# Input projection of a two-layer hybrid block on one core: seven block products for eight on half of the contraction, convolved q and k through DRAM

## The chip, the cores and the metric

The kernel runs on one core of a Trainium2 chip. The metric is the device time of one execution in microseconds. Before the change three runs gave 1715.57, 1718.47 and 1721.88 us, median 1718.47 us.

## The reference, cut to what matters

Two layers are computed. In each, 1024 latent tokens and 256 context tokens (width 1024) are normalised and modulated, then multiplied by one input projection whose columns feed three groups: bidirectional gated DeltaNet heads (q, k, v, each through a 5-tap convolution over the tokens and a SiLU), latent attention heads, and a short convolution branch. Outputs are gated, concatenated and sent through one output projection.

```python
hx = modulate(x, norm_g, shift_x, scale_x)
hc = modulate(ctx, norm_g, shift_c, scale_c)
(xq, xk, xv, xz_a, xb, xa, xq_a, xkv_a, xz_b, xh, xbg, xcg, xz_c) = split_in(hx @ w_in)
(cq, ck, cv, cz_a, cb, ca, cq_a, ckv_a, cz_b, ch, cbg, ccg, cz_c) = split_in(hc @ w_in)
...
qkv = jax.nn.silu(dwconv_centred(jnp.concatenate([q, k, v], axis=-1), conv_w))
...
c_x = conv_branch(xh, xbg, xcg, xz_c, conv_w)
```

All of it is float32. The second layer computes context tokens only where keys, values and k are needed.

## The kernel before

**Operands.** A float32 product is made of three products of rounded parts (hi·hi, hi·lo, lo·hi). The tokens stand transposed in `hg` as hi and lo, in three groups (`GROUPS`: 512, 512 and 256 tokens), with the contraction of 1024 as 8 tiles of 128 (`KD`). The weights come in blocks of 128 output columns: `load_w` fetches one block (512 KB), `split_w` makes its hi on ScalarE (`split`, L75) and its lo on VectorE (L76).

**Blocks.** After 10 small tiles for the narrow columns (`mla_tile`) and two gate blocks (`z2`), `run_blocks` goes through a list `bl` of 24 blocks: k (4 heads), q (4), the convolution branch (2 x 4 parts: h, c gate, b gate, z), v (4), and four gate blocks. `Block.mm(g)` runs 24 matmuls into one PSUM bank for a token group; `post0` takes the banks (copy into a padded row `pad`, convolution `conv` as one ScalarE and four VectorE passes, SiLU), and `post1`, two blocks later, transposes the heads and stores them. Weight tiles `w` have two buffers (tag W8); the next but one block is split while the next is multiplied. Convolved q and k of all heads stay in SBUF (`KQ`).

**Background lanes.** Beside the blocks run generators on the kernel's own clock `Sched`: each 8 matmuls advance it by `tick(0.0034 * n)`, and a lane is resumed when its next due time has passed, so that a `yield` is rounded up to the next tick. `start_prep` (hook at block 4) makes the decay matrices and k·k per token tile, `start_base` (5) inverts small blocks in a long run of small VectorE operations (L680, L681), `start_prep_q` (9) makes q·k, `start_merge` (8) assembles inverses in ten `merge` generators on two workers, and `start_kv` (21) prepares the latent keys, `kv_lane`, once all ten are merged. The block phase ends at

```python
sch.until(lambda: len(kvf) == NT)
```

(L1037), after which the attention phase is written, with TensorE's order fixed by hand: the key rows are spread by DMA (`key_rope`, L1058), and attention (`a_max`, `a_scores`, `a_pv`) is interleaved with the two recurrences `recur`, whose inputs come through a DMA ring, while q and k are read from `KQ`. Outside that stretch the order on each engine comes from a planner that takes what is ready by its place in the program; every DMA is issued by SyncE (SP) in order.

**Buffers.** Tags share slots: B16 (7), B4 (2), W8 (2), T5 (5 rows of 1288), P4 (4), P2 (7); PSUM has 8 banks (`bank`). A tile whose tag has no free slot waits for one.

## Time and profile before

| | before |
|---|---|
| median of three runs | 1718.47 us |
| profiled execution | 1723.55 us, span 1721.8 us |
| mean granted TensorE clock | 0.978 of 2.4 GHz |
| busy share: TensorE, VectorE, ScalarE, GpSimd | 96%, 64%, 44%, 38% |
| block phase, first layer | 121 to 552 us of the span |
| block phase, second layer | 1000 to 1378 us |

The first stretch of the span loads and modulates the tokens, and after each block phase come attention with the recurrences (552 to about 815 us and 1378 to about 1622 us) and the output projection. A busy share is an average over these stretches. A matmul's listed duration overlaps its neighbours', so the pace of matmuls is read from chains of them and not from the mean duration.

### The profile page before, as it was taken

How to read it: one execution, taken by the hardware profiler on the slowest of the kernel's cores; microseconds unless marked ns; L12 is line 12 of the kernel's file. 1: busy time of each engine (PE TensorE's matmuls, PEld its weight loads, DVE VectorE, ACT ScalarE, POOL GpSimd, SP SyncE). 2: the span in 40 equal slices, each digit the busy share in tenths (PEclk: the TensorE clock that was granted, in tenths of full speed). 3: DMA queues.
4: the chain of work that ended last, by engine and by line, in shares of the span. 5: the costliest groups of instructions: out<-in, count | busy, mean ns of one | idle time of the engine just before them, and what ended most of it. 6: DMA issues, size and time to landing. Idle time of an engine off the chain costs nothing.

```text
span 1721.8 us, 29896 instructions
## 1 busy us (share of the span) xinstructions
PE 1650.5 (96%) x10964; PEld 1316.9 (76%) x10964; DVE 1101.9 (64%) x2041; ACT 758.8 (44%) x1909; POOL 646.3 (38%) x848
## 2 busy tenths in 40 slices
PE   7999999999999999998999999999999989999998
PEld 5887888787887877764888887787778778776586
DVE  2534668878643767765565346689797377776664
ACT  4644565223444534344354435652245444434432
POOL 0520345321320456557331212544232136556731
PEclk8999999999999899999999999999999989999999
DMA  9332464753254755544443314556524465454551
GB/s 360 124 126 79 155 196 150 242 178 123 78 160 125 257 157 177 186 144 159 132 141 111 104 56 134 161 179 224 166 70 128 151 211 164 160 188 156 172 159 49
DMA packets 195403, 266.54 MB, mean 155 GB/s; under 512 B 50529, under 2 KB 115249, under 8 KB 195257
## 3 DMA queue, kind: packets, MB, share of 16 engines
q1 hardware_dynamic: 195256, 264.64, 47.8%
q8 instruction: 87, 1.43, 0.3%
q14 instruction: 60, 0.48, 0.1%
HBM read 182.71 MB, written 79.17 MB: 152 GB/s over the span
## 4 chain that ended last, share of the span: by engine, by line
PE 68%; DVE 10%; DMA 9%; issue 5%; ACT 3%; POOL 3%; SPq 1%; POOLq 0%; DVEq 0%; ACTq 0%
PE bank L452 26%; PE bank L84 22%; PE bank L1159 3%; PE bank L1236 2%; PE bank L1255 2%; PE bank L1249 2%; DVE pr L680 2%; PE bank L1254 2%; PE bank L1102 2%; DMA gcb<-row_d 2%; DVE Mb L681 1%; DMA wa<-in_w_ada_dram 1%; PE bank L1226 1%; DVE acc L466 1%; PE bank L516 1%
## 5 line engine op out<-in xcount | busy, mean ns | idle before, releaser
L452 PE MATMUL bank<-h_hi,w 128*128 128x512 f32 x1664 | 432.5, 403 | 2.4 <-DVE h_hi L283 2.4
L452 PEld LDWEIGHTS bank<-h_hi,w 128*128 128x128 f32 x1664 | 305.4, 190 | 74.6 <-issue 4.5
L452 PE MATMUL bank<-h_lo,w 128*128 128x512 f32 x832 | 217.7, 402 | 0.0
L452 PEld LDWEIGHTS bank<-h_lo,w 128*128 128x128 f32 x832 | 154.3, 189 | 37.0 <-issue 1.6
L466 DVE SCALAR_TENSOR_TENSOR acc<-pad,col,acc 128x1284 f32<-128x1284 f32 (+1 forms) x104 | 160.1, 1540 | 11.1 <-ACT acc L463 9.5
L1129 POOL TENSOR_TENSOR vt<-vt,probT 128x512 f32<-128x512 f32 x110 | 144.7, 1335 | 20.2 <-ACT probT L1143 19.5
L84 PE MATMUL bank<-wo_hi,mix 128*128 128x512 f32 x576 | 145.0, 402 | 1.8 <-ACT wo_hi L75 1.1
L1143 ACT ACTIVATE probT<-bank 128x512 f32<-128x512 f32 (+1 forms) x168 | 96.5, 590 | 98.2 <-PE bank L84 92.2
L84 PEld LDWEIGHTS bank<-wo_hi,mix 128*128 128x128 f32 x576 | 108.2, 191 | 28.6 <-ACT wo_hi L75 2.6
L76 DVE TENSOR_TENSOR w<-wr,w 128x1024 fp32r<-128x1024 f32 x52 | 66.6, 1283 | 93.3 <-ACT w L75 93.3
L1104 DVE TENSOR_REDUCE mx<-bank 128x1 f32<-128x512 f32 (+1 forms) x200 | 108.5, 585 | 10.9 <-PE bank L1102 9.7
L452 PE MATMUL bank<-h_c,w 128*128 128x256 f32 x816 | 109.7, 287 | 0.0
L452 PEld LDWEIGHTS bank<-h_c,w 128*128 128x128 f32 x816 | 102.2, 190 | 5.8 <-issue 3.7
L75 ACT ACTIVATE w<-wr 128x1024 fp32r<-128x1024 f32 x52 | 54.9, 1060 | 75.3 <-PE bank L452 56.3
L84 PE MATMUL bank<-qt,kh 97*128 97x512 f32 (+1 forms) x256 | 84.4, 411 | 3.5 <-ACT probT L1143 2.8
L1159 PE MATMUL bank<-probT,vt 128*64 128x512 f32 (+1 forms) x336 | 79.4, 594 | 0.0
L1232 POOL TENSOR_TENSOR ring<-ring,qx 128x512 f32<-128x512 f32 x32 | 40.9, 1277 | 92.7 <-DMA ring<-row_d 76.8
L680 DVE TENSOR_TENSOR pr<-L,Mb 128x31 f32<-128x31 f32 (+15 forms) x186 | 70.7, 380 | 4.6
L84 PE MATMUL bank<-wo_lo,mix 128*128 128x512 f32 x288 | 73.5, 395 | 0.0
L681 DVE TENSOR_TENSOR Mb<-Mb,pr 128x31 f32<-128x31 f32 (+15 forms) x186 | 68.6, 369 | 5.0
L617 POOL TENSOR_TENSOR gcb<-gcb,gc 128x1024 f32<-128x1024 f32 x20 | 44.5, 2231 | 62.7 <-DMA gcb<-row_d 36.8
L79 ACT ACTIVATE pad<-bank 128x512 f32<-128x512 f32 (+1 forms) x78 | 41.0, 531 | 54.1 <-PE bank L452 39.1
(310 smaller groups left out, 3225.2 us busy)
## 6 DMA issues: line engine op xcount, KB each, us to landing
wr<-in_w_blk_dram SPq DMA_DIRECT2D x52, 512.0 KB
wa<-in_w_ada_dram SPq DMA_DIRECT2D x32, 512.0 KB
gcb<-row_d SPq DMA_DIRECT2D x20, 512.0 KB
nn_d<-N SPq DMA_DIRECT2D x20, 512.0 KB
ring<-vr_d SPq DMA_DIRECT2D x40, 256.0 KB
ring<-nn_d SPq DMA_DIRECT2D x40, 256.0 KB
qk_d<-gcb SPq DMA_DIRECT2D x18, 512.0 KB
ring<-kt_d SPq DMA_DIRECT2D x36, 256.0 KB
```

What stands on the lines that cost most here:

```text
L75: A.activation(out=hi, in_=raw, func=ACTF.Copy)
L76: eng.tensor_tensor(out=lo, in0=raw, in1=hi.bitcast(F32), op=ALU.subtract)
L84: T.matmul(outp, lhsT=lh, rhs=rh, start=q == 0, stop=q == n - 1)
L452: T.matmul(pb[:, 0:n], lhsT=self.w[:, wi, k, :], rhs=hg[g][hi][:, k, :], start=q + k == 0, stop=q == 2 and k == KD - 1)
L466: V.scalar_tensor_tensor(out=acc[:, 2:hi], in0=pad[:, 2 + t - r:hi + t - r], scalar=col[:, ci:ci + 1], in1=acc[:, 2:hi], op0=ALU.mult, op1 ...
L617: P.tensor_tensor(gcb, gcb, bc(gc[:, i, :], 128), ALU.subtract)
L680: V.tensor_tensor(out=pv, in0=bc(L[:, 0:k, k], w), in1=N[:, k:k + 1, k:32].to_broadcast([128, k, w]), op=ALU.mult)
L681: V.tensor_tensor(out=N[:, 0:k, k:32], in0=N[:, 0:k, k:32], in1=pv, op=ALU.subtract)
L1104: V.tensor_reduce(mx[:, gk:gk + 1], pb[:, 0:n], AX.X, ALU.max)
L1129: P.tensor_tensor(acc, a0, a1, ALU.add)
L1143: A.activation(out=pts[r][:, kk, 0:n], in_=pb, func=ACTF.Exp)
L1159: T.matmul(u["po"][64 * r:64 * r + 64, 0:n], lhsT=vx[:, kt, hh * 64:hh * 64 + 64], rhs=pts[r][:, kk, 0:n], start=kt == keys[0], stop=kt == ...
```

## The change

Blocks are taken in pairs (`run_pairs`). For token groups 0 and 1 and contraction tiles 0 to 3, the two blocks and two groups make a 2 by 2 by 2 block product, computed with seven products of 6 matmuls instead of eight. Sums of the tokens (`make_sums`, t1 to t4, in the slots of the narrow weights) are made once a layer, sums of the weights (`weight_sums`) once a pair; partial results go through PSUM banks and are added into SBUF rows (`add`, on VectorE, and two GpSimd adds). Tiles 4 to 7 and the context group stay as they were. A pair has three weight tiles (b0.w, ws, b1.w) in the two W8 slots; b0's lo is made on GpSimd, raw weights move to tag B4. The ticks are now `0.00255 * n` each 6 matmuls. Convolved q and k are stored to DRAM (`kx_d`, `qx_d`) and loaded again in `prep`, `prep_q`, before attention (`KQ`, two loads of eight tiles) and, for one step, in `recur`. The second merge worker starts only after all three base batches in both layers.

```diff
+        def weight_sums(a, b):
+            ws = st([128, 2, KD, 128], "W8", F32R, name="ws")
+            s1 = st([128, 2, 2, 128], "P2", name="sr")
+            s2 = st([128, 2, 2, 128], "P2", name="sr")
+            P.tensor_tensor(s1[:, 0], b[:, 0:2], b[:, 2:4], ALU.add)
+            P.tensor_tensor(s1[:, 1], s1[:, 0], a[:, 0:2], ALU.subtract)
+            P.tensor_tensor(s2[:, 0], a[:, 0:2], b[:, 0:2], ALU.subtract)
+            P.tensor_tensor(s2[:, 1], a[:, 2:4], s1[:, 1], ALU.subtract)
+            for q, s in enumerate((s1, s2)):
+                split(s.rearrange("p a b f -> p (a b) f"), ws[:, 0, 4 * q:4 * q + 4], ws[:, 1, 4 * q:4 * q + 4], P)
+            return ws
...
+        def run_pairs(blocks, hooks):
...
+                b0.open(b0.padded)
+                z = bank()
+                chain(z, prod(b0.w, 2, sm["b21"]) + b0.std(0))
+                copy_a(b0.dst(0), z)
+                ws = weight_sums(b0.raw, b1.wr)
+                b0.raw = None
+                if b0.n_tok == TOK:
+                    b0.mm(2)
+                x = bank()
+                chain(x, prod(b0.w, 0, sm["b11"]))
+                b0.add(0, x)
+                copy_a(b0.dst(1), x)
+                y = bank()
+                chain(y, b0.std(1), stop=False)
+                x = bank()
+                chain(x, prod(ws, 2, sm["t2"]))
+                b0.add(1, x)
+                with tc.high_priority(offset=300):
+                    b1.split()
...
+                chain(y, prod(ws, 6, sm["b22"]), False)
+                late(q - 1)
+                b1.open(b1.padded)
+                x = bank()
+                chain(x, prod(ws, 4, sm["t3"]))
+                b1.add(0, x, b0.dst(1))
+                b0.add(1, y)
+                x = bank()
+                chain(x, prod(ws, 0, sm["t1"]))
+                copy_a(b1.dst(1), x)
+                P.tensor_tensor(b0.dst(1), b0.dst(1), b1.dst(1), ALU.add)
+                P.tensor_tensor(b1.dst(1), b1.dst(1), b1.dst(0), ALU.add)
+                b0.post0(b0)
+                hook(q + 1)
+                if b1.n_tok == TOK:
+                    b1.mm(2)
+                y = bank()
+                chain(y, b1.std(0) + prod(b1.w, 2, sm["t4"]))
+                b1.add(0, y)
+                if nxt:
+                    with tc.high_priority(offset=300):
+                        nxt[0].raw = nxt[0].wr
+                        nxt[0].split(P)
+                else:
+                    load_qkv()
+                y = bank()
+                chain(y, b1.std(1))
+                b1.add(1, y)
+                late(q)
+                b1.post0(b1)
...
-                    if first or (len(based) >= (2 if last else 3) and free.ok("ada", "q")):
+                    if first or (len(based) == 3 and free.ok("ada", "q")):
...
+        for nm, src, n_kq in (("k", kx_d, 8), ("q", qx_d, 8)):
+            KQ[nm] = st([128, 8, 4, 128], "B16", name=nm + "x")
+            S.dma_start(out=KQ[nm], in_=src[0:8].rearrange("i p h t -> p i h t"))
         kh = st([128, 4, 1024], "B16", F32R, name="kh")
```

## Rows read from the trace of the kernel before

**Rows 1.** The page: busy time, share and instructions; then costliest groups.

```profile
PE 1650.5 (96%) x10964; PEld 1316.9 (76%) x10964; DVE 1101.9 (64%) x2041; ACT 758.8 (44%) x1909; POOL 646.3 (38%) x848
...
L452 PE MATMUL bank<-h_hi,w 128*128 128x512 f32 x1664 | 432.5, 403 | 2.4 <-DVE h_hi L283 2.4
...
L452 PE MATMUL bank<-h_lo,w 128*128 128x512 f32 x832 | 217.7, 402 | 0.0
...
L1129 POOL TENSOR_TENSOR vt<-vt,probT 128x512 f32<-128x512 f32 x110 | 144.7, 1335 | 20.2 <-ACT probT L1143 19.5
...
L76 DVE TENSOR_TENSOR w<-wr,w 128x1024 fp32r<-128x1024 f32 x52 | 66.6, 1283 | 93.3 <-ACT w L75 93.3
...
L75 ACT ACTIVATE w<-wr 128x1024 fp32r<-128x1024 f32 x52 | 54.9, 1060 | 75.3 <-PE bank L452 56.3
```

**Rows 2.** Both block phases: stretch, length, busy per engine, clock, DMA share, GB/s.

```profile
121.00:552.00 431.00, 424.46 (x3351) 344.89 (x3348) 279.33 (x481) 187.59 (x469) 119.49 (x187) 1.00 0.47 146
1000.00:1378.00 378.00, 367.30 (x2829) 294.90 (x2827) 266.52 (x458) 174.81 (x429) 118.14 (x189) 0.98 0.46 143
```

**Rows 3.** The chain that ended last: start, us, what.

```profile
555.04 5.30 DMA kc<-pes
...
957.41 9.33 PE bank L452 x40
...
1387.93 4.80 DMA ring<-nn_d
```

**Rows 4.** Second block phase in stretches of 10 us; columns as in rows 2.

```profile
1150.00:1160.00 10.00, 10.00 (x53) 8.42 (x52) 9.55 (x22) 3.90 (x17) 3.74 (x7) 1.00 0.64 194
...
1190.00:1200.00 10.00, 6.48 (x54) 5.30 (x53) 8.19 (x18) 3.53 (x8) 4.16 (x11) 0.71 0.56 172
...
1210.00:1220.00 10.00, 7.96 (x39) 6.67 (x39) 9.46 (x23) 1.53 (x3) 0.00 (x0) 0.66 0.39 116
```

**Rows 5.** VectorE in the first block phase (180 to 550 us), groups by shape.

```profile
L653 DVE TENSOR_TENSOR gcb<-bank,gcb 128x512 f32<-128x512 f32 x20 | 12.8, 681 | 0.1
```

**Rows 6.** VectorE in the second block phase, groups by shape.

```profile
L466 DVE SCALAR_TENSOR_TENSOR acc<-pad,col,acc 128x1284 f32<-128x1284 f32 x32 | 49.6, 1551 | 5.1 <-ACT acc L463 4.5
L76 DVE TENSOR_TENSOR w<-wr,w 128x1024 fp32r<-128x1024 f32 x22 | 29.2, 1327 | 37.3 <-ACT w L75 37.3
L466 DVE SCALAR_TENSOR_TENSOR acc<-pad,col,acc 128x1024 f32<-128x1024 f32 x20 | 26.6, 1330 | 1.2 <-ACT acc L463 0.9
```

**Rows 7.** L680, then L681, alone in the second block phase (VectorE busy).

```profile
1000.00:1378.00 378.00, 35.13 (x93) 0.98 0.46 143
...
1000.00:1378.00 378.00, 34.19 (x93) 0.98 0.46 143
```

**Rows 8.** GpSimd's L617 over the span: ns least, median, most.

```profile
L617 POOL TENSOR_TENSOR gcb<-gcb,gc x20: 1892/1930/3088, 193.3 to 1164.2; 128x1024 f32<-128x1024 f32 x20
```

**Rows 9.** Timeline of GpSimd, then VectorE, 1162 to 1168 us.

```profile
1164.17 3.00 POOL L617 TENSOR_TENSOR gcb<-gcb,gc 128x1024 f32<-128x1024 f32 x1
...
1162.35 0.40 DVE L680 TENSOR_TENSOR pr<-L,Mb 128x247 f32<-128x247 f32 x1
...
1164.13 1.28 DVE L466 SCALAR_TENSOR_TENSOR acc<-pad,col,acc 128x1024 f32<-128x1024 f32 x1
...
1166.14 1.30 DVE L680 TENSOR_TENSOR pr<-L,Mb 128x240 f32<-128x240 f32 x1
```

**Rows 10.** SyncE timeline: last inverse stored, first key rows spread, each layer.

```profile
532.45 0.32 SPq L760 DMA_DIRECT2D nn_d<-N  x1
...
547.62 1.91 SPq L1058 DMA_DIRECT2D kh<-pes  x2
...
1357.57 6.38 SPq L760 DMA_DIRECT2D nn_d<-N  x2
...
1376.64 1.87 SPq L1058 DMA_DIRECT2D kh<-pes  x2
```

**Rows 11.** Around both ends of the block phase; columns as in rows 2.

```profile
555.00:560.00 5.00, 1.94 (x11) 1.29 (x9) 4.88 (x10) 3.75 (x8) 3.87 (x4) 0.92 1.01 311
560.00:565.00 5.00, 4.53 (x18) 4.22 (x19) 3.44 (x9) 2.27 (x6) 4.38 (x4) 0.50 0.96 334
...
1370.00:1375.00 5.00, 5.00 (x30) 4.18 (x29) 3.09 (x8) 3.18 (x9) 0.00 (x0) 1.00 0.22 50
```

More of the change, by code (lines that the diff above doesn't have):

```diff
@@ L438, in __init__ @@
                 self.c0, self.n_tok, self.post0, self.post1 = c0, n_tok, post0, post1
-                self.ps = {}
-            def load(self):
-                self.wr = load_w(l, self.c0)
-            def split(self):
-                self.w = split_w(self.wr)
-            def mm(self, g):
-                t0, n = GROUPS[g]
-                pb = bank()
-                for q, (wi, hi) in enumerate(((0, 0), (0, 1), (1, 0))):
-                    for k in range(KD):
-                        T.matmul(pb[:, 0:n], lhsT=self.w[:, wi, k, :], rhs=hg[g][hi][:, k, :], start=q + k == 0, stop=q == 2 and k == KD - 1)
-                    sch.tick(0.0034 * n)
-                self.ps[g] = pb
+                self.padded = not (c0 >= O_ZA and c0 < O_AB or c0 >= O_ZB and c0 < O_H)
@@ new lines, in load, with split, std @@
+            def load(self, tag="P4"):
+                self.wr = load_w(l, self.c0, tag)
+            def split(self, eng=V):
+                self.w = split_w(self.wr, eng)
+                self.wr = None
+            def mm(self, g):
+                n = GROUPS[g][1]
+                pb = bank()[:, 0:n]
+                chain(pb, self.std(g, range(KD)))
+                copy_a(self.dst(g), pb)
+            def std(self, g, ks=range(4, KD)):
+                return [(self.w[:, wi, k, :], hg[g][hi][:, k, :]) for wi, hi in ((0, 0), (0, 1), (1, 0)) for k in ks]
@@ new lines, in prod, with m, hook, late @@
+        def prod(w, k0, mv):
+            def m(i, k):
+                return mv[:, i, k, :] if not isinstance(mv, list) else mv[i][:, k, :]
+            return [(w[:, wi, k0 + k, :], m(hi, k)) for wi, hi in ((0, 0), (0, 1), (1, 0)) for k in range(2)]
+        def run_pairs(blocks, hooks):
+            n = len(blocks)
+            def hook(q):
+                if q in hooks:
+                    hooks[q]()
+            def late(q):
+                if q >= 0 and blocks[q].post1:
+                    blocks[q].post1(blocks[q])
+            sm = SUMS
+            for q in range(0, n, 2):
+                hook(q)
+                b0, b1 = blocks[q:q + 2]
+                nxt = blocks[q + 2:q + 4]
+                b0.open(b0.padded)
[18 more added lines that the diff above has]
+                if nxt:
+                    nxt[0].load("B4")
+                    nxt[1].load("B4")
+                chain(y, prod(ws, 6, sm["b22"]), False)
[17 more added lines that the diff above has]
+                b1.add(0, y)
+                if nxt:
+                    with tc.high_priority(offset=300):
[8 more added lines that the diff above has]
+                b1.post0(b1)
+            late(n - 1)
@@ L640, in prep_q @@
             S.dma_start(out=E, in_=e_d[i])
+            kk, qq = (st([128, 4, 128], "P2", name="kk") for _ in range(2))
+            S.dma_start(out=kk, in_=kx_d[i])
+            S.dma_start(out=qq, in_=qx_d[i])
             yield
@@ L763 @@
         batches = ((6, 7, 8, 9), (0, 1, 2, 3), (4, 5))
[L764 to L782 removed]
+        merges = [(i, bt, i - (6, 0, 2)[bt]) for bt in range(3) for i in batches[bt]]
         qkv = {}
@@ L1022, in worker @@
                 while todo_m:
-                    if first or (len(based) >= (2 if last else 3) and free.ok("ada", "q")):
-                        yield from todo_m.pop(0)
+                    if first or (len(based) == 3 and free.ok("ada", "q")):
+                        yield from merge(*todo_m.pop(0), "P4" if first else "T5")
                     else:
```

229 lines of the change are left out of this document (116 added, 113 removed).

## The prediction, written before the result

> **What bounds the kernel now.** I read the page first. TensorE is busy 96% of the span and no other engine passes 64% [rows 1], which suggests TensorE but says nothing of the phase that is changed, so I cut that phase out: in the two block phases TensorE is busy 424.5 of 431 us and 367.3 of 378 us [rows 2]. The reader is to see that almost nothing is idle there: whatever shortens TensorE's own list of matmuls shortens the phase, if it stays fed. Then the chain of waits, for the pace: 40 matmuls of 512 columns follow each other in 9.33 us [rows 3], 0.233 us each; the listed 402 ns overlap. Last, in 10 us stretches, who is next in line. In the second layer VectorE is busy 9.55 of 10 us at 1150 us and 9.46 at 1210 us, and where TensorE falls to 6.48 or 7.96 the clock is granted at 0.71 and 0.66 [rows 4], so part of such a stretch ran at the lower level (1.2 GHz). VectorE is already a second bound there.
>
> **What the change removes.** A pair has 2 blocks x 2 groups x 24 = 96 matmuls of 512 columns; after, 48 for contraction tiles 4 to 7 and 7 products x 6 = 42, so 90. Twelve pairs in two layers save 24 x 6 = 144 of the 2496 that rows 1 count (1664 + 832). 144 x 0.233 = **33.6 us**; 144 x 0.402 would say 58, which is the trap of the listed duration. At best all of it comes; it is nothing where TensorE waits instead.
>
> **What it adds on VectorE.** Six adds of a bank into SBUF a pair; nearest row 0.68 us [rows 5]: +4.1. One weight split less, -1.28 [rows 1]. Net +2.8 x 12 = 34 us a layer; the branch's part 2 and 3 products move to GpSimd (2 x 2 parts x 2 groups x 0.68 = -5.4), the token sums cost nine passes of 1024, 9 x 1.28 = 11.5 (an estimate by the weight split, of the same size). **+40 us a layer**: 279.3 becomes 319 of 414 us (431 - 16.8), and 266.5 becomes 306.5 of 361 us (378 - 16.8). No total is exceeded, but the crowded stretch of rows 4 is. TensorE has 8 banks to run ahead in, so I charge 4 us; nothing if the inversions of L680 and L681 simply slide.
>
> **What it adds on GpSimd.** At 1.335 us for 512 columns [rows 1], scaled by width: b0's lo 2.6, four sums of 256 2.6, two lo of 512 2.6, two adds 2.6, so 10.4 a pair, with four products of the branch some **135 us a layer** on top of 119. That is 254 of 414 and 253 of 361 us: it fits, and costs nothing while TensorE covers it. What it costs the neighbour is the third rival.
>
> **Weight tiles.** Three share two slots. b1.w may only be written when b0's last matmul is through, and is wanted 24 matmuls later: 24 x 0.233 = 5.6 us of cover. ScalarE needs 1.06 and VectorE 1.28 [rows 1], with one convolution pass of 1.55 [rows 6] in flight 3.9 us. ws has z, x and y (36 matmuls, 8.4 us) and the next b0.w 30 matmuls (7 us) for 1.06 + 2.6. All fit: 0 us. If the cover fails by 1.5 us each pair, 24 x 1.5 = 36 us.
>
> **ScalarE and DMA.** Extra copies and SiLU passes fall on an engine at 187.6 of 431 us [rows 2]: hidden. kx and qx are stored (5.2 MB a layer) and read again in prep (2.6), prep_q (5.2), KQ (4.2) and once in recur (1): about 18 MB beside the 63 MB of a block phase (431 us x 146 GB/s [rows 2]). Share 0.47 becomes about 0.6; hidden, though each load also stands in SP's order ahead of weights and may wait there for a P2 slot.
>
> **The seams.** Two things move to the end of the block phase.
> First, KQ: 2 x 2.1 MB issued ahead of the key rows in SP's order; q waits for the last use of t4, about 12 matmuls (2.8 us) before the end. In the first layer the DMA engines are full there (1.01 and 0.96 at 311 and 334 GB/s) and the key rows end TensorE's wait [rows 3, 11]; 2.1 MB at 0.32 MB per us is 6.5 us. In the second they are nearly empty (0.22) [rows 11]. Bounds 0 and 13; I take 5, most of one load.
> Second, the lanes. Before, the last inverse is stored at 532 and 1358 to 1363 us and the key rows follow at 548 and 1377 [rows 10], at the phases' very end: the lanes are just in time. I counted their yields on the kernel's own clock. Before: blocks end at 313.3 ticks and kv_lane at 313.3; second layer 271.6 and 273.6; the last merge at 297.7 and 259.4, which at 431/313 = 1.38 and 378/272 = 1.39 us a tick is 531 and 1361 us, agreeing with rows 10. After, a tick is 1.31 and not 1.74, a yield of 3.0 rounds up to 3.9 and not 3.5, the blocks have 16 ticks fewer, and the second worker starts later in the second layer. The count gives 297.7 and 305.7 in the first layer, **255.9 and 305.9** in the second: four merges and the kv lanes then stand behind the last block. The first layer owes at most 8 x 1.38 = 11 us; I take 3, since the kv lanes need no merge's data. In the second the 50 ticks are not 50 us, since a tick without block matmuls takes no time of its own; only the merges' chains of small steps remain. Four merges on two workers are two rounds of 5.2 + 4 x 3.9 = 21 ticks. For the upper bound I let a round last as long as under load: a tick's own matmuls are worth 0.233/0.2176 = 1.07 us (the 0.2176 is what a matmul of 512 columns advances the clock), so 2 x 21 x 1.07 = 45 us. From that comes off what the lanes no longer cost inside the phase: a tick took 1.39 us, of which 0.32 was other work, and 48 ticks of it, 15 us, move past the end. Upper bound 30. Below, 0: attention's first matmuls read no inverse, and the planner may put them first. I take 6, near the lower end for that reason.
>
> **Sum**: -33.6 + 4 + 5 + 3 + 6 = **-15.6 us**. Against the profiled execution (1723.55 us, of which 1721.8 is the span) that is 1708; it stands 5.1 us above the median of the runs, so 1702.9: **1703 us**, 0.9% faster.
>
> **Rivals.**
> *Lost at the seams, same time.* The second layer's lanes cost their bound, 30 for 6: 1703 + 24 = 1727; half of that difference gives 1715. For it: rows 10 show no slack before, and the count adds 48 ticks. Against: only order holds attention behind the merges, and the planner takes what is ready. Centre 1715; it decides where the lanes cost 13 us and not 6, which brings 1710, half a per cent under the median.
> *GpSimd and VectorE block each other, slower.* L617 has a least of 1.89 us [rows 8]; at 1164.17 it took 3.00 while VectorE's L466, which began just before, ran to 1165.41, and the L680 begun at 1166.14 took 1.30 instead of 0.40 and ended only after L617 did [rows 9]. So one holds the other up for the rest of an operation. The Trainium skill says so (SBUF — State Buffer, "Who interferes with whom"): a VectorE instruction with two SBUF inputs and a GpSimd one that reads SBUF exclude each other, and the later fully blocks. By that rule, and rows 9 agree, work moved from VectorE to GpSimd is not free. The price: in the second layer VectorE's passes of that kind are 49.6 + 26.6 + 29.2 [rows 6] and 35.1 + 34.2 [rows 7], 175 of 378 us, 46%. If VectorE waits out 46% of the 135 us added, it needs 306.5 + 62 = 368.5 us, which at the 95% that it reaches in rows 4 is 388 us: that phase ends 27 us later than in my sum, **1730 us**, and with the lanes at their bound 1754. It decides from the point where VectorE bears (0.95 x 361 - 306.5)/135 = 27% of the added time; banks are then emptied late and matmuls wait at the lower clock. Against: GpSimd may bear the waits, and the first layer has room (319 + 62 = 381 of 414).
> *All hidden*: 1718.5 - 33.6 = 1685, the lower end of the first case.
>
> **Chances and range.** Forecast (1686 to 1710): 0.48. Seams: 0.24. Blocking: 0.28. Half a per cent, 8.6 us, is about what a measurement tells from no change; so faster 0.48, same 0.24, slower 0.28. The forecast's own range is 1686 to 1710; the range that should hold 8 in 10 reaches to the other cases and stops at 1738, leaving out the blocking case with its late lanes.
>
> **What the profile after would show.** Right: 2352 matmuls of 512 columns in the projection, both phases some 15 us shorter with TensorE still above 96% busy, the clock at 1.00, and a wait of a few us on DMA where KQ is loaded. Seams: nn_d stores after the last projection matmul and TensorE idle ahead of the key rows in the second layer. Blocking: L466 and the GpSimd sums far above 1.55 and 1.335 us, TensorE waiting for `add` or `ws`, and the clock below 0.95 between 1150 and 1300 us. Weight tiles: TensorE idle before the first matmul of b1.w or ws in every pair. I am wrong most simply if VectorE becomes the clock of the second block phase.

## The result, and the profile after

The changed kernel takes **1921.64 us** (median of 4 runs, 1918.63 to 1923.05) against 1718.8 us for the kernel before on the same chip: ratio 1.1178, 95% interval 1.1153 to 1.1203. That is 202.8 us slower, where 15 faster were forecast, and outside the range. The profiled execution has a span of 1916.9 us (1721.8 before) at a mean clock of 0.928 (0.978). All times below are medians; one execution of e8 took 7108.9 us against 1855.6 to 1863.5 in its other three, and is left out.

The page of the changed kernel, busy time, share and instructions, answers to [rows 1]:

```profile
PE 1669.2 (87%) x10820; PEld 1325.5 (69%) x10820; DVE 1297.3 (68%) x2155; ACT 804.4 (42%) x1961; POOL 967.2 (50%) x1116
```

The 144 matmuls are gone (10964 before), and yet TensorE is busy 19 us longer, some 52 us more than with the forecast's saving of 33.6, at the lower mean clock. VectorE has 195 us more and GpSimd 321. TensorE's idle time is 248 us against 71. So of the 195 us between the two spans, 176 are idle time and 19 are busy time.

The same span cut at each layer's first and last block matmul and its first key score (stretch, length, busy per engine with instructions, clock, DMA share, GB/s):

```profile
50.00:624.00 574.00, 495.42 (x3667) 402.53 (x3666) 394.01 (x577) 246.04 (x587) 304.11 (x390) 0.93 0.48 152
624.00:640.50 16.50, 9.26 (x41) 6.97 (x39) 9.99 (x24) 8.43 (x21) 1.26 (x1) 0.79 0.77 246
640.50:1027.40 386.90, 366.57 (x1996) 283.88 (x1997) 250.81 (x497) 163.17 (x416) 185.25 (x166) 0.96 0.50 160
1027.40:1537.80 510.40, 418.51 (x2581) 340.29 (x2584) 375.52 (x527) 200.99 (x461) 283.67 (x361) 0.90 0.44 139
1537.80:1585.00 47.20, 28.56 (x576) 23.27 (x576) 21.71 (x53) 29.47 (x87) 14.92 (x29) 0.60 0.59 176
```

Cut in the same way, the other kernels give the lengths below. A block phase runs from first to last block matmul (rows 2 cut it later, behind the narrow tiles), a seam from there to the first key score, and l0 attention from there to the second layer's first block matmul, output projection included; l0 and l1 are the layers.

| us | l0 blocks (TensorE busy) | l0 seam | l0 attention | l1 blocks (TensorE busy) | l1 seam |
|---|---|---|---|---|---|
| before | 500.2 (492.0) | 5.3 | 376.9 | 443.7 (431.4) | 5.6 |
| after | 574.0 (495.4) | 16.5 | 386.9 | 510.4 (418.5) | 47.2 |
| e1 next pair | 554.5 (495.7) | 15.7 | 386.2 | 501.8 (424.5) | 47.1 |
| e5 sums on VectorE | 537.8 (494.4) | 16.0 | 385.6 | 465.7 (411.9) | 46.4 |
| e7 place, no weight work | 520.7 (484.9) | 15.9 | 384.3 | 439.4 (408.1) | 48.5 |
| e17 and no inversion | 507.9 (480.2) | 16.5 | 390.0 | 420.8 (399.5) | 43.2 |
| e10 before, no inversion | 495.3 (490.4) | 5.3 | 375.3 | 428.3 (424.9) | 5.6 |

The block phases lost 73.8 + 66.7 = 140.5 us, the seams 11.2 + 41.6, the first layer's attention 10.0; the first and last stretches gave back 8.2. The second layer's block phases don't hold the same work: 618 matmuls fewer run in the changed one (2581 against 3199), of which 72 are the saving; the others are mostly small ones of the merges, and the seam behind it holds 576 matmuls for 23. The block phases of the kernel before, columns as above:

```profile
51.60:551.80 500.20, 492.03 (x3759) 402.42 (x3758) 306.59 (x542) 224.59 (x573) 142.25 (x255) 1.00 0.45 142
934.00:1377.70 443.70, 431.44 (x3199) 354.05 (x3197) 290.39 (x511) 207.35 (x515) 134.63 (x254) 0.98 0.44 139
```

TensorE's waits in the changed kernel, by what ended them (total, times, longest):

```profile
PE bank L645 <- ACT acc L627: 105.6, 12, 12.4
PE bank L476 <- ACT ws L75: 25.8, 7, 13.1
PE bank L190 <- DMA wa<-in_w_ada_dram: 13.5, 6, 6.6
PE bank L842 <- issue: 9.1, 3, 4.8
PE bank L958 <- DMA mq<-mla_d: 8.9, 3, 5.4
```

All 12 waits of the first line stand at one place: `late(q)`, the transposes of a k, q or v pair's first block, directly behind `b1.std(1)` in the program. One of them in order of time (start, length, engine, line):

```profile
241.01 0.59 ACT L79 ACTIVATE pad<-bank 128x512 f32<-128x512 f32 x1
242.65 2.40 POOL L76 TENSOR_TENSOR w<-wr,w 128x1024 fp32r<-128x1024 f32 x1
245.00 1.29 POOL L579 TENSOR_TENSOR pad<-pad 128x512 f32<-128x512 f32 x1
246.32 1.37 ACT L608 ACTIVATE acc<-pad,col 128x1284 f32<-128x1284 f32 x1 [3.72 <-DMA gcb<-row_d]
247.73 4.66 DVE L611 SCALAR_TENSOR_TENSOR acc<-pad,col,acc 128x1284 f32<-128x1284 f32 x2 [5.64 <-ACT acc L608]
248.33 2.71 POOL L736 TENSOR_TENSOR gcb<-gcb,gc 128x1024 f32<-128x1024 f32 x1 [0.84 <-DMA gcb<-row_d]
249.74 1.10 PE L476 MATMUL bank<-h_hi,w 128*128 128x512 f32 x4
252.31 1.75 DVE L737 TENSOR_TENSOR gcb<-gcb 128x512 f32<-128x512 f32 x1
254.59 2.09 DVE L611 SCALAR_TENSOR_TENSOR acc<-pad,col,acc 128x1284 f32<-128x1284 f32 x1
257.80 3.48 DVE L611 SCALAR_TENSOR_TENSOR acc<-pad,col,acc 128x1284 f32<-128x1284 f32 x2
259.95 0.63 ACT L75 ACTIVATE ws<-sr 128x512 fp32r<-128x512 f32 x1 [0.62 <-POOL sr L518]
260.60 1.28 ACT L627 ACT_TABLE_LOAD   x1
261.90 1.27 ACT L627 ACTIVATE acc<-acc 128x1284 f32<-128x1284 f32 x1
263.22 1.12 PE L645 MATMUL bank<-cst,acc 128*128 128x128 f32 x4 [12.39 <-ACT acc L627]
```

The chain copy, GpSimd add, scaled copy, four passes, SiLU takes 22 us (241.0 to 263.2). It waits for GpSimd, which is at the next weight's split until 245.0; its first two passes take 4.66 us together beside GpSimd's L736, where 104 such passes of the kernel before take 1.54 each in the mean; and the lanes' L737 stands between the second and the third. (The row at 257.80 holds the fourth pass and the first one of the pair's other block.) Before the SiLU, ScalarE copies a weight sum and loads a table. TensorE's other matmuls are through at 250.8. In the same way, the chains of all 12 waits take 15 to 23 us from copy to SiLU (19 in the mean), for 6 to 17 us of matmuls (10 in the mean); and in 17 of the 24 pairs L579 starts at the moment at which another GpSimd operation ends, in 14 of them the split of the next weight.

The clock around this wait, in stretches of 5 us (columns as above):

```profile
245.00:250.00 5.00, 5.00 (x32) 3.91 (x33) 2.24 (x2) 2.16 (x3) 4.04 (x7) 1.00 0.80 205
250.00:255.00 5.00, 0.83 (x4) 0.35 (x2) 5.00 (x4) 0.00 (x0) 5.00 (x4) 0.90 0.49 187
255.00:260.00 5.00, 0.00 (x0) 0.00 (x0) 4.97 (x5) 1.41 (x2) 4.80 (x7) 0.50 0.22 66
260.00:265.00 5.00, 1.78 (x9) 1.78 (x10) 3.21 (x3) 3.77 (x5) 5.00 (x6) 0.50 0.16 50
265.00:270.00 5.00, 5.00 (x22) 4.15 (x22) 4.93 (x3) 3.58 (x21) 4.33 (x2) 0.73 0.59 186
```

TensorE stands idle and its clock is granted at 0.50, the lower level (1.2 GHz); when it is busy again, from 263.2 us on, the clock stays there at first. That is how a wait also lengthens the matmuls behind it.

Five theories of the loss were tested. Before the first run: **A**, the place of these transposes; **B**, GpSimd's new work holds up VectorE; **C**, the seams are a cost of their own; **D**, the way of q and k through DRAM; from the fifth run on also **E**, VectorE simply has too much to do. A band is the range of times that an expectation gives to a theory. Added lines shift the numbers by 1 to 5, so that L645 is L646, L649 or L650 in some runs.

### The profile page after: what moved, and what is told of

Its sections match the earlier page's. It is cut to its first block, busy times and chain, and to the rows that moved or that the text cites. A ratio compares the mean times of both kernels' runs of the same rounds, so it can differ in the third digit from the quotient of the medians.

```text
span 1916.9 us, 30443 instructions
## 1 busy us (share of the span) xinstructions
PE 1669.2 (87%) x10820; PEld 1325.5 (69%) x10820; DVE 1297.3 (68%) x2155; ACT 804.4 (42%) x1961; POOL 967.2 (50%) x1116
## 5 line engine op out<-in xcount | busy, mean ns | idle before, releaser
L476 PE MATMUL bank<-h_hi,w 128*128 128x512 f32 x1088 | 313.1, 411 | 0.0
L476 PEld LDWEIGHTS bank<-h_hi,w 128*128 128x128 f32 x1088 | 206.4, 196 | 47.7 <-issue 3.3
L476 PE MATMUL bank<-h_lo,w 128*128 128x512 f32 x544 | 163.9, 410 | 0.0
L1232 POOL TENSOR_TENSOR vt<-vt,probT 128x512 f32<-128x512 f32 x110 | 143.6, 1324 | 27.1 <-ACT probT L1246 26.3
L455 DVE TENSOR_TENSOR pad<-bank,pad 128x512 f32<-128x512 f32 x144 | 97.7, 683 | 85.0 <-POOL pad L580 25.8
L645 PE MATMUL bank<-cst,acc 128*128 128x128 f32 x232 | 42.9, 350 | 105.6 <-ACT acc L627 105.6
L476 PEld LDWEIGHTS bank<-h_lo,w 128*128 128x128 f32 x544 | 103.9, 195 | 26.0 <-issue 1.6
L645 PEld LDWEIGHTS bank<-cst,acc 128*128 128x128 f32 x232 | 36.5, 183 | 111.6 <-ACT acc L627 110.3
L476 PE MATMUL bank<-h_c,w 128*128 128x256 f32 x816 | 110.4, 288 | 1.0 <-ACT jk L657 1.0
L476 PEld LDWEIGHTS bank<-h_c,w 128*128 128x128 f32 x816 | 103.7, 191 | 5.3 <-ACT jk L657 1.5
L803 DVE TENSOR_TENSOR Mb<-Mb,pr 128x31 f32<-128x31 f32 (+15 forms) x186 | 102.3, 550 | 4.7
L476 PE MATMUL bank<-wm_hi,ws 128*128 128x512 f32 x288 | 80.5, 411 | 22.2 <-ACT ws L75 22.1
L76 POOL TENSOR_TENSOR ws<-sr,ws 128x512 fp32r<-128x512 f32 x48 | 74.9, 1572 | 19.7 <-ACT ws L75 19.7
```

The source lines that it names most:

```text
L76: eng.tensor_tensor(out=lo, in0=raw, in1=hi.bitcast(F32), op=ALU.subtract)
L455: V.tensor_tensor(out=self.dst(g), in0=pb, in1=self.dst(g) if to is None else to, op=ALU.add)
L476: T.matmul(pb, lhsT=lh, rhs=rh, start=start and q == 0, stop=stop and q == len(prs) - 1)
L645: T.transpose(pt[:, i * 128:(i + 1) * 128], src(i0 + i), ident)
L803: V.tensor_tensor(out=N[:, 0:k, k:32], in0=N[:, 0:k, k:32], in1=pv, op=ALU.subtract)
L1232: P.tensor_tensor(acc, a0, a1, ALU.add)
```

## The experiments

### e1: the transposes in the next pair

```diff
+                late(q - 2)
                 late(q - 1)
...
-                late(q)
                 b1.post0(b1)
+            late(n - 2)
```

> The changed kernel with one edit: the transposes of a pair's first block stand in the next pair, ahead of those of the second block, instead of directly behind the pair's own last product. Theory A (the place of these transposes): the stalls of TensorE in front of them, 105.6 us in the changed kernel's trace, go, and of the 52 us that its matmuls last longer than before (1669.2 busy, against 1650.5 less 33.6 for the 144 matmuls saved) a part goes with them: 1764 to 1816 us. Theory B (GpSimd and VectorE hold each other up, so that VectorE's chain is the pace): the same work has still to be done on the same engines, TensorE waits elsewhere (banks, weights): above 1870 us. Theory C (the seams at the phases' ends): what the stalls were is C's business no more; the second layer's tail of some 35 us and the first layer's 5 us stay in either case.

1890.88 us, ratio 1.0990 (1.0964 to 1.1016): 30.8 less than the changed kernel, not A's 105 to 157, and in B's band. The stall shrank from 105.6 to 29.4 us, but less than half of that reached the time:

```profile
PE bank L476 <- ACT ws L75: 29.6, 9, 7.2
PE bank L646 <- ACT acc L628: 29.4, 4, 10.3
```

A is real and small. TensorE's idle time fell by 36.5 us (247.7 to 211.2), so that half of what it no longer waits here it waits elsewhere, and it is busy 9 us longer (1678.2 us).

### e2: the old kernel with its transposes a block earlier

```diff
-                    if n_g == 0 and q > 1 and blocks[q - 2].post1:
-                        blocks[q - 2].post1(blocks[q - 2])
+                if q > 0 and blocks[q - 1].post1:
+                    blocks[q - 1].post1(blocks[q - 1])
```

> The kernel before with one edit: the transposes of each k, q and v block stand directly behind the matmuls of the next block (some 14 us of cover), instead of one group into the block after that. Theory A in its plain form (the place alone makes the stall): its chain of copies, four passes of 1.54 us and SiLU is about 12 us where nobody disturbs it, so that a queue on VectorE of a few us makes stalls of 0 to 5 us at up to 24 blocks: 1740 to 1800 us. If the time stays within 1% of 1718.5, one block is cover enough for the old chain, and what made the stalls in the changed kernel is the place together with the longer chain there (adds on GpSimd, waits for t1's product). Theory B expects no change, since no work is moved to GpSimd.

1723.07 us, ratio 1.0022 (1.0008 to 1.0035). One block, some 14 us of matmuls, is cover enough for the old chain of about 12 us. The changed kernel has both less cover and a longer chain; this run doesn't say what the old chain would cost behind 10 us.

### e3, e5, e7: GpSimd's weight work

e3 and e7 leave a part of the computation out: they take `ws = b0.w` for the sums, so that the third weight tile goes too, and split `nxt[0]` on VectorE. e5 computes everything and moves all of the weight work to VectorE. e5 and e7 have e1's edit too. From e5:

```diff
-            P.tensor_tensor(s1[:, 0], b[:, 0:2], b[:, 2:4], ALU.add)
+            V.tensor_tensor(out=s1[:, 0], in0=b[:, 0:2], in1=b[:, 2:4], op=ALU.add)
...
-                        nxt[0].split(P)
+                        nxt[0].split(V)
```

> The changed kernel with GpSimd's weight work taken out: the four weight sums and their split are left out (the products of the sums run with the first block's own weights, the same number of matmuls), and the split of the next pair's first weight runs on VectorE. It leaves out part of the computation. GpSimd loses about 10 of its 13 us a pair; the third weight tile goes too. Theory B: VectorE's passes are no longer held up and most of the loss goes: below 1800 us. Theory A: the transposes stay behind the same four passes, adds and SiLU; only the 25.8 us of waits for the sums' split and the stretched passes go (104 x 0.15 us): the time stays above 1850 us, and the stalls ahead of the transposes above 70 us.

> The changed kernel with the transposes in the next pair (as in the first experiment, 1890.9 us) and, in addition, all of GpSimd's weight work on VectorE: the four sums of 256, their two splits, the split of the next pair's first weight. VectorE gets some 4.3 us a pair more (two of 0.69, one of 1.28, four of about 0.4), 24 x 4.3 = 102 us in all. Theory B (what hurts is that GpSimd's passes hold VectorE's up): the inversion's passes fall back from 532 and 550 towards 380 and 369 ns, 62 us, the convolution's from 1694 towards 1540, 16 us, the waits for the sums' split (29.6 us) go: 1830 to 1870 us. Theory E (VectorE has too much to do in the block phases, whoever causes it): its load only grows: 1885 to 1930 us.

> The changed kernel with the transposes in the next pair and GpSimd's weight work taken out (the four sums and their split are left out, the products of the sums run with the first block's own weights; the split of the next pair's first weight on VectorE): it leaves out part of the computation. It asks whether the two causes add up. The place alone gave 30.7 us and the weight work alone 76.4 us; in the run without the weight work 70 us of stalls ahead of the transposes were left. If place and GpSimd's work together are the loss inside the block phases, these 70 us and some cold matmuls go as well: 1745 to 1785 us, and what stays above 1720 is the seams (some 53 us). If a third cause is there (VectorE's plain load, the DMA way of q and k), above 1800 us.

e3: 1845.18 us, 1.0722 (1.0700 to 1.0744); e5: 1840.89, 1.0685 (1.0662 to 1.0708); e7: 1798.41, 1.0461 (1.0436 to 1.0485). e5 hit B's band: against e1 VectorE has 24 us more to do in all (1330.8 against 1306.7 busy) and the kernel is 50 us faster. The inversion's passes fell from 583 and 599 ns in e1 to 447 and 444 (532 and 550 in the changed kernel, 380 and 369 before); but GpSimd's adds no longer queue behind a split either, and the run doesn't part the two. E alone is out. The passes in e5:

```profile
L803 DVE TENSOR_TENSOR pr<-L,Mb 128x31 f32<-128x31 f32 (+15 forms) x186 | 83.2, 447 | 3.6
L804 DVE TENSOR_TENSOR Mb<-Mb,pr 128x31 f32<-128x31 f32 (+15 forms) x186 | 82.6, 444 | 3.7
```

e3 fell between the bands: 70.0 us of waits ahead of the transposes stayed. e7 did too, at the edge of the one for a third cause (above 1800): place and weight work give 123.2 us together, 16 more than one by one.

### e4: q and k through DRAM, alone on the old kernel

```diff
                         A.activation(out=KQ[nm][s][:, h, :], in_=acc[:, p0:p0 + n], func=ACTF.Silu)
+                        S.dma_start(out=(kx_d if nm == "k" else qx_d)[t0 // 128:(t0 + n) // 128, :, h, :].rearrange("i p t -> p i t"),
+                                    in_=KQ[nm][s][:, h, :].rearrange("p (i t) -> p i t", t=128))
...
+            kk = st([128, 4, 128], "P2", name="kk")
+            S.dma_start(out=kk, in_=kx_d[i])
```

> The kernel before with one part of the change alone: convolved q and k are also written to DRAM, the preparation lanes read them from there, and both are loaded back for the first 8 tiles ahead of the key rows at the end of the blocks (here into the tiles that hold them already). The prediction charged this 5 us, with bounds of 0 and 13. Theory A and B: 1718 to 1732 us. Theory D (the way through DRAM itself costs much, by full DMA queues or by loads that wait in SP's order): above 1760 us.

1745.64 us, ratio 1.0149 (1.0128 to 1.0169): 26.1 us, five times the charge and between the bands. It doesn't lie at the seam, which is 5.4 and 5.6 us as before, but at the start of the preparation lanes:

```profile
PE bank L631 <- DMA kk<-kx_d: 27.2, 5, 11.2
```

The lane starts behind the last k block, and its matmul stands in TensorE's order while k is stored and loaded. In the changed kernel waits of this kind are 1.9 us only; they come out as other stalls go (11.3 us in e1, 15.9 in e7), so that the 26.1 us can't simply be added to the other costs.

### e6, e8, e13: the seams

e6:

```diff
-                    sch.tick(0.00255 * n)
+                    sch.tick((0.0032 if last else 0.00255) * n)
...
-            S.dma_start(out=KQ[nm], in_=src[0:8].rearrange("i p h t -> p i h t"))
...
         key_rope()
+        for nm, src in (("k", kx_d), ("q", qx_d)):
+            S.dma_start(out=KQ[nm], in_=src[0:8].rearrange("i p h t -> p i h t"))
```

e8 is e5 with these edits. e13 instead:

```diff
-                    if first or (len(based) == 3 and free.ok("ada", "q")):
-                        yield from merge(*todo_m.pop(0), "P4" if first else "T5")
+                    if first or (len(based) >= (2 if last else 3) and free.ok("ada", "q")):
+                        yield from merge(*todo_m.pop(0), "P4" if first or last else "T5")
```

> The changed kernel with edits to the seams alone: q and k are loaded behind the key rows and not ahead of them, and in the second layer a group of six matmuls advances the kernel's own clock by 0.0032 n and not 0.00255 n, so that the lanes are through 25% earlier. Theory C (the seams cost by themselves): from the last block matmul to the first key score the first layer goes from 16.5 to about 10 us, the second from 47.2 to 10 to 20, and the block phases stay as they are: 1880 to 1900 us. Rival: the lanes' work only moves back into a phase that is crowded already, the second block phase (510.4 us) grows by what the seam gives back, and the time stays within 1% of 1921.6.

> All edits that keep the whole computation together: the transposes in the next pair, the weight work on VectorE, q and k loaded behind the key rows, the faster clock of the lanes in the second layer. Sum of the single expectations by theories B and C: 1790 to 1840 us; by theory E 1870 to 1920 us. No theory expects it under the 1718.5 us of the kernel before.

> The changed kernel with one edit: in the second layer the second merge worker starts as before the change, when two of the three inverses are there and not three (its working tile then lies where the first worker's does). On the kernel's own clock the last key lane then ends at 281.9 and not at 305.9 ticks, for blocks that end at 255.9. Theory C (that late start makes the second layer's seam): from the last block matmul to the first key score 47.2 becomes 20 to 28 us, 1895 to 1908 us. Rival (as in the sixth run, what leaves the seam lengthens the block phase by as much): within 0.7% of 1921.6 us.

e6: 1919.69 us, 1.1157 (1.1129 to 1.1185); e8: 1858.62, 1.0802 (1.0778 to 1.0826), 18 slower than e5 and between its bands; e13: 1917.09, 1.1150 (1.1125 to 1.1174). The second layer's block phase and seam in e13:

```profile
1027.80:1550.30 522.50, 428.97 (x2874) 348.49 (x2872) 373.61 (x537) 210.74 (x492) 285.71 (x373) 0.89 0.45 141
1550.30:1583.20 32.90, 17.27 (x272) 13.53 (x272) 17.03 (x42) 19.81 (x56) 8.78 (x16) 0.74 0.54 162
```

The seam is 14.3 us shorter and the phase 12.1 longer; in e6 27.1 and 20.1. Both runs hit their rivals' bands, and C falls as a cost of its own: the late merges are work that no longer fits beside the blocks, and earlier it costs three quarters as much or more. e6 holds two edits, and its loads behind the key rows moved a wait: the first seam is 5.2 us shorter, but TensorE waits 11.6 us for `nn_d` in the recurrences (2.0 in the changed kernel), and the first layer's attention takes 398.4 us for 386.9.

### e9, e10, e15: the inversion's passes left out

```diff
...
-                V.tensor_tensor(out=pv, in0=bc(L[:, 0:k, k], w), in1=N[:, k:k + 1, k:32].to_broadcast([128, k, w]), op=ALU.mult)
-                V.tensor_tensor(out=N[:, 0:k, k:32], in0=N[:, 0:k, k:32], in1=pv, op=ALU.subtract)
```

All three leave a part of the computation out. e15 has e1's edit as well.

> The changed kernel with the two VectorE passes of every step of the base inversion left out (186 pairs of passes, 201.3 us of VectorE in the changed kernel's trace): it leaves out part of the computation, and the place and length of the first block's own chain stay as they are. Theory E (VectorE's load in the block phases is what the loss hangs on): most of 201 us comes back, the kernel is at 1740 to 1790 us. Theory A (the chain ahead of the transposes by itself): the waits of 105.6 us stay for the greater part, 1850 to 1900 us. Between 1790 and 1850 us both hold by half.

> Control: the kernel before with the same passes left out (139.3 us of VectorE; it leaves out part of the computation). TensorE was busy in 424.5 of 431 and 367.3 of 378 us of its block phases, so that theories A and E both expect nearly nothing: 1700 to 1719 us. If it falls by more, the old kernel hung on VectorE too, and the first run shows less.

> The changed kernel with the transposes in the next pair and, in addition, the inversion's passes left out (part of the computation is left out). The place alone gave 30.7 us and the passes alone 49.9. If chain and VectorE's load are two limits of which the longer one shows (each hides behind the other), the two together give more than their sum, 80.6: 1770 to 1830 us. If they are independent costs: 1835 to 1850 us. If GpSimd's weight work is a limit by itself (waits for the sums' split, 29.6 us in the first run) the gain is smaller: above 1850 us.

e9: 1871.75 us, 1.0897 (1.0871 to 1.0922). The passes took 201.3 us, VectorE is busy 186 us less (1111.5 for 1297.3), and 49.9 come back; VectorE is busy 55% of the first block phase, and the stall stays nearly whole:

```profile
PE bank L645 <- ACT acc L627: 102.1, 12, 13.9
```

So the stall isn't a VectorE without time; it fits the length of a chain of dependent steps, of which GpSimd's steps and queue are still a part here. e10: 1700.72 us, 0.9894 (0.9875 to 0.9914); the old kernel gave 19.9 us for the same edit, the most that its expectation allowed. e15: 1827.00, 1.0615 (1.0582 to 1.0649): 94.6 against 80.6 for the two edits one by one, at the edge of its first band; chain and load hide behind each other only a little.

### e11, e16: the added work alone on the old kernel

```diff
                     blocks[q + 2].split()
+                    for r in range(5):
+                        scr = st([128, 2, 128], "sm", name="scr")
+                        P.tensor_tensor(scr, blocks[q + 2].wr[:, r:r + 2], blocks[q + 2].wr[:, r + 2:r + 4], ALU.add)
```

e16 has four sums, on VectorE.

> The kernel before with GpSimd work of the size of the change's and nothing else of it: for each block whose weights are split in the loop, five sums of 256 columns into a scratch tile that nobody reads, some 5 x 1.05 = 5.3 us a block, 5.3 x 22 = 116 us a layer (the prediction put the change's at 135). It measures the prediction's third rival by itself. Theory B: VectorE's passes are held up as in the changed kernel (inversion from 380 and 369 towards 530 and 550 ns, convolution from 1540 towards 1690), and the second layer's phase is some 27 us longer: 1735 to 1770 us. Rival (held up passes are no matter as long as no chain waits for GpSimd): within 1% of 1718.5 us, though the passes are longer.

> The kernel before with VectorE work of the size of the change's net addition and nothing else of it: for each block whose weights are split in the loop, four sums of 256 columns into a scratch tile that nobody reads, some 0.4 us each, 1.6 us a block, 22 x 1.6 = 35 us a layer (the prediction put the change's at 40 and charged 4 us for both layers). If that charge is right: 1718 to 1727 us. If VectorE is the second bound already, in the second layer above all: 1735 to 1760 us.

e11: 1762.89 us, ratio 1.0252 (1.0230 to 1.0275), 42.3 us. VectorE's groups of the inversion in the kernel before (count, busy, mean ns, idle before), then VectorE's and GpSimd's in e11, then both block phases (columns as above):

```profile
L680 DVE TENSOR_TENSOR pr<-L,Mb 128x31 f32<-128x31 f32 (+15 forms) x186 | 70.7, 380 | 4.6
L681 DVE TENSOR_TENSOR Mb<-Mb,pr 128x31 f32<-128x31 f32 (+15 forms) x186 | 68.6, 369 | 5.0
```

```profile
L680 DVE TENSOR_TENSOR pr<-L,Mb 128x31 f32<-128x31 f32 (+15 forms) x186 | 84.9, 457 | 14.5 <-POOL scr L780 6.4 <-DVE Mb L681 0.5
L681 DVE TENSOR_TENSOR Mb<-Mb,pr 128x31 f32<-128x31 f32 (+15 forms) x186 | 84.2, 452 | 4.8
L780 POOL TENSOR_TENSOR scr<-wr 128x256 f32<-128x256 f32 x220 | 203.6, 950 | 88.6 <-DVE Mb L681 25.3 <-issue 24.8 <-PE bank L381 18.5
```

```profile
51.80:569.40 517.60, 497.08 (x3759) 405.89 (x3758) 323.30 (x542) 224.30 (x573) 244.90 (x365) 0.99 0.44 137
950.90:1419.60 468.70, 436.65 (x3199) 356.54 (x3197) 316.57 (x511) 207.91 (x515) 244.16 (x364) 0.96 0.42 132
```

GpSimd's 204 us, whose results nobody reads, lengthen the inversion's passes from 380 and 369 ns in the kernel before to 457 and 452 and the phases by 17.4 and 25.0 us. The 121 of the 372 passes that overlap a GpSimd operation on two tensors in this trace are 255 ns longer than passes of the same shape that don't. 6.4 us of it are this run's own: its scratch tile shares slots with the inversion. VectorE is busy 41.8 us more (1143.7 for 1101.9); at e16's rate that would cost some 12 us (an estimate), so that longer passes alone hardly make the 42.3. That the lanes' own GpSimd steps queue behind the sums is a rival that no run parts from it. e16: 1739.59 us, 1.0112 (1.0084 to 1.0140): 68.7 us of plain VectorE work cost 19.1. e11 hit B's band and e16 that of VectorE as a second bound.

### e12, e14: what was put together

e12 is e5 with the two adds of L579 and L580 on VectorE, the preparation lanes half a pair later, and the loads of q and k behind the key rows. e14 is e7 with e13's edit and these loads.

```diff
-                P.tensor_tensor(b0.dst(1), b0.dst(1), b1.dst(1), ALU.add)
+                V.tensor_tensor(out=b0.dst(1), in0=b0.dst(1), in1=b1.dst(1), op=ALU.add)
...
-        run_pairs(bl, {4: start_prep, 5: start_base, 9: start_prep_q, 8: start_merge, 21: start_kv})
+        run_pairs(bl, {5: start_both, 9: start_prep_q, 8: start_merge, 21: start_kv})
```

> The whole computation, with all that helped or should help: the transposes in the next pair, the weight work and the two adds between the blocks' halves on VectorE, the preparation lanes started half a pair later (so that no matmul waits for k's way through DRAM, 8.9 us in the fifth run), q and k loaded behind the key rows (5 us of the first layer's seam in the sixth). From the fifth run's 1840.9 us: less 9, less 5, and the adds are worth -10 (a shorter chain) to +10 (36 us more for VectorE): 1815 to 1840 us. It isn't expected under 1718.5 us.

> The sum of the causes: transposes in the next pair, weight work left out (the four sums and their split; part of the computation is left out, as in the seventh run, 1798.4 us), second merge worker early in the second layer, q and k loaded behind the key rows. If place, GpSimd's work and seams are all there is and add up: 1798.4 less 20 to 25 less 5, 1765 to 1775 us, and what stays over 1718.5 less 33.6 is the way through DRAM (27.1 us alone) and VectorE's added load. If what leaves the seam comes back in the phase: 1785 to 1800 us.

e12: 1855.21 us, 1.0788 (1.0766 to 1.0811), 14 more than e5; e14: 1812.76, 1.0540 (1.0512 to 1.0568), 14 more than e7. e14 leaves the weight work out, as e7 does. Both missed their bands, and they share a cost: with the loads behind the key rows TensorE waits 23.6 and 23.7 us for `nn_d` in the recurrences, and the first layer's attention takes 400.0 and 398.5 us (385.6 in e5, 384.3 in e7). Besides, what e14's second seam gave back against e7 (20.2 us) its second block phase took for the most part (14.9). e5 stays the fastest version that computes everything.

### e17, e18: three causes away

e17 is e7 without the inversion's passes; e18 starts its preparation lanes half a pair later. Both leave a part of the computation out.

> The changed kernel with three causes taken away at once: the transposes in the next pair, the weight work left out (the four sums and their split), the inversion's passes left out (both leave out part of the computation). By the single runs (place 30.7, weight work 76.4, the two together 123.2, passes 49.9, and 14.0 more for passes and place together): 1734 to 1749 us. To be held against the kernel before without the passes, 1700.7 us: what it stays above 1700.7 less 33.6 is the second layer's late merges (41 us in the trace) and the way through DRAM (27.1 us alone). If a cause is left that no run has touched: above 1755 us.

> The same, and the preparation lanes start half a pair later, so that the load of convolved k has time to come back from DRAM before a matmul stands waiting for it (15.9 us of such waits in the seventh run). Theory D (that wait is the price of the way through DRAM): 10 to 16 us less than the run before it. Rival (the lanes, started later, are later at the phases' ends by as much, with most of the second layer's merges behind the last block already): within 5 us of it.

e17: 1763.31 us, 1.0250 (1.0220 to 1.0280), 14 above its band and in the range that the expectation gives to a cause which no run has touched. e18: 1755.67, 1.0210 (1.0181 to 1.0240): 7.6 less, between the two expectations. The two block phases of e10, the old kernel without the same passes, then of e17:

```profile
51.50:546.80 495.30, 490.40 (x3759) 400.81 (x3759) 238.88 (x356) 225.18 (x574) 140.43 (x255) 1.00 0.46 144
927.40:1355.70 428.30, 424.94 (x3199) 348.10 (x3197) 226.70 (x325) 208.63 (x515) 136.85 (x254) 1.00 0.46 144
```

```profile
50.00:557.90 507.90, 480.23 (x3666) 391.93 (x3666) 304.83 (x402) 231.92 (x565) 212.16 (x307) 0.98 0.54 172
964.40:1385.20 420.80, 399.54 (x2583) 328.42 (x2587) 274.81 (x352) 187.69 (x437) 181.29 (x278) 0.98 0.54 170
```

TensorE's busy time goes from 915.3 to 879.8 us. That isn't the saving yet, since the second phase of e17 also lacks some 540 small matmuls of the merges. The block products by themselves (L452 in e10, L476 in e17; stretch, length, busy with matmuls, clock, DMA share, GB/s) show it:

```profile
51.50:546.80 495.30, 392.47 (x1872) 1.00 0.46 144
927.40:1355.70 428.30, 334.05 (x1440) 1.00 0.46 144
```

```profile
50.00:557.90 507.90, 373.74 (x1800) 0.98 0.54 172
964.40:1385.20 420.80, 313.96 (x1368) 0.98 0.54 170
```

They are busy 687.7 us for 726.5, 38.8 less for 144 matmuls. But the phases together are 5.1 longer, for 48.9 us idle against 8.3; 16.0 of that is the wait for k out of DRAM, 15.9 the transposes. Of the rest of the 64.9 us between the two spans, the seams are 48.8 (11.2 and 37.6), the first layer's attention 14.7.

## Why the prediction was wrong

**Saving, 33.6 us**: right. 144 matmuls are gone, and with three causes taken away the block products are busy 38.8 us less (e17 against e10). In the changed kernel little of it shows: TensorE is busy 9.5 us less in the two block phases (923.4 against 913.9), though the merges' small matmuls left the second one too, at clocks of 0.93 and 0.90 for 1.00 and 0.98, and idle time went from 20.4 to 170.5.

**The step that failed first is one that isn't in the sum.** The prediction priced engines by their totals and never set the first block's chain against its own transposes, which now come in the same pair. The chain shown is 22 us for some 9.8 us of matmuls behind the copy (19 and 10 in the mean of the 12), and TensorE stood 105.6 us there. That was not the price of the place, though: moving it gave 30.8 us in the changed kernel and 46.8 once the weight work was gone (e7 against e3).

**GpSimd, "it fits, and costs nothing"**: the largest mis-sized term. 135 us a layer were charged nothing; 162 and 149 came in the block phases (the 135 us leave out the token sums, of which five passes run on GpSimd). Without the weight work the changed kernel is 76.5 us faster (e3), and 102 us a layer of unread sums cost the old kernel 42.3 (e11). The rival in which GpSimd and VectorE block each other (the "third rival" of the text, second in its list) had the place right, and passes beside GpSimd are longer as it said: it gave 27 us for the second layer, e11 measured 25.0, and 17.4 in the first, to which the prediction left room; that the sizes agree is partly luck, since e11 has three quarters of the work. It was still no forecast of 1921, for it saw GpSimd as a thief of VectorE's time and not as a link of the chain. By the Trainium skill (SBUF — State Buffer, "Who interferes with whom") a VectorE instruction with two inputs in SBUF excludes a GpSimd one that reads there; the rows of e11 agree, with 457 ns for 380.

**VectorE, 4 us**: too low. 40 us a layer were expected, 87 and 85 came in the block phases: the inversion's passes alone went from 139.3 to 201.3 us. Plain work of 69 us costs 19.1 us on the old kernel (e16), and leaving out 201 us of passes gives back 49.9 (e9). The condition named at the end, VectorE as the clock of the second phase, was not met: it is busy 74% there, and without the inversion's passes the stall stays.

**Weight tiles, 0 us**: 25.8 us of waits for `ws`. What came last was ScalarE's copy of the sums, which GpSimd makes four in a row; but with the sums on VectorE (e5) 20.0 us of such waits stay, so GpSimd's pace alone doesn't explain them.

**DRAM**: 18 MB and "hidden" was right for the traffic and wrong for the wait: 26.1 us alone, at the preparation lanes' start, which no sentence named. At the first seam 5 us were taken; the seam grew by 11.2, of which 5.2 go when the loads stand behind the key rows (e6).

**Lanes, 3 and 6 us**: the count was right (the merges stand behind the last block) and the size wrong. The second seam grew 41.6 us, above the bound of 30 and near the 45 before the deduction; the 15 us that the phase should have given back don't show in a phase that is 66.7 us longer. Part of the seam ran at half the clock. TensorE in stretches of 5 us there (columns as above):

```profile
1555.00:1560.00 5.00, 0.33 (x25) 0.36 (x29) 1.75 (x5) 2.58 (x10) 3.02 (x7) 0.50 0.22 40
1560.00:1565.00 5.00, 4.36 (x128) 3.95 (x120) 0.57 (x2) 3.77 (x12) 0.27 (x1) 0.50 0.12 33
```

But it is hardly a separate cost: a faster clock for the lanes and an earlier second worker mostly moved it into the phase (e6, e8, e13). The seams rival had this place right; its 1715 took the bound as the worst, and the block phases as won.

**The account.** Alone on the old kernel, the additions cost 26.1 + 42.3 + 19.1 = 87.5 us; less the 33.6 saved, 54 of 202.8 are shown that way. This sum is rough: e11 and e16 carry only a part of the added work, and the costs partly hide one another. From the other side, taking place, weight work and inversion out gives back 158.3, of which 19.9 the old kernel gives too. The other 149 us no addition shows alone. Some 42 us are the second seam, which no run on the old kernel has. The chain and its stall appear only where the additions stand together in a pair; that they make up the rest is argued, not shown, and no single edit holds it. **Left open**: why most of the second seam's cost comes back wherever its lanes run, and the first layer's attention, 10 us longer in the changed kernel and 5 or more in all its versions but not with DRAM alone (e4: 378.0, against 376.9 before); there TensorE is busy 7 us longer at a mean clock of 0.96 for 0.98, and idle 3 us longer, where the recurrence waits 2.8 us for the step that it loads from `kx_d`.

## What to carry to other kernels

Saving 6% of the block products pays only if TensorE does not wait longer for what the saving needs. Before costing added work by totals, write down for each unit of the pipeline the longest chain of dependent steps and the matmuls that stand between its start and its consumer; here 15 to 23 us against about 10. An idle GpSimd doesn't make work on it free: price that work by running it, unread, in the old kernel, and then look at which chain has to wait for it.

## What the runs showed of the hardware

GpSimd sums that nobody reads lengthened VectorE's small passes by 20% (e11), and the kernel became 50 us faster when the weight work went from GpSimd to the busier VectorE (e5). A stall costs twice: the 232 transposes of the line at which TensorE stalls (L645) have a median of 374 ns, 273 before, and the clock around one stall went from 1.00 to 0.50. In the last two stretches shown, at the second seam, TensorE is busy 4.36 of 5 us and still granted 0.50, the lower level (1.2 GHz), behind 5 us in which it was busy 0.33.
